# Mixing stage: w_out takes the unnormed attention outputs half by half, the token factors meet its products, and the values, tasks and places are ordered anew

## The chip, the cores and the metric

The kernel runs on one core of one Trainium2 chip. The metric is the device time of one execution in microseconds (us), as a median of several runs. PE is the matrix engine (PEld its weight loads), DVE the vector engine, ACT the activation engine, POOL the general engine, and SP issues most of the DMAs.

## What is computed

A model of five blocks, 512 tokens by 1024 features, batch 1, all in float32. The first block is the one that the change touches: a feed-forward part (ffn1), a mixing part, a second feed-forward part (ffn2), and a gated projection of a side input p (PLE). The mixing part is:

```python
u = rms_norm(h, g_mix_pre)
q_a, k_a, v_a, q_b, k_b, v_b = split(u @ w_in)          # each 512 wide, 8 heads of 64
o_a = stick_breaking_attention(q_a, k_a, v_a)
o_b = chunk_band_attention(q_b, k_b, v_b, rel_bias)
mixed = concat([rms_norm(o_a, g_out_sb), rms_norm(o_b, g_out_ch)])
h = h + rms_norm(mixed @ w_out, g_mix_post)
```

`rms_norm(o, g)` multiplies each token by one number, 1/rms over the 512 features, and each feature by its gain. Four more blocks follow (convolution, attention with forget gates, gated delta rule, sliding window); neither version differs in them.

## The kernel before

Activations lie transposed, features on the 128 partitions and 512 tokens along them, so a 1024-wide activation is eight tiles of 128x512. Every large product is made of blocks of 128x128 weights. Both sides are split into a high and a low part of the type fp32r, and a block costs three matmuls: high by high, low weights by high, high weights by low. Weights come in chunks of four blocks (256 KB) through four staging buffers `wst`; ACT makes the high part, DVE the low part. 82 places of 128x512 (`slots`) hold all other tiles, eight PSUM banks the products.

The order of all instructions is set while the program is built, by a planner in the kernel. The main line is written as plain code (`gemm`, `vproj`, `gemm_two`); the attentions are generators (`sb_pair`, `ch_pair`, each for two heads, four of each) that yield what they wait for. Between two blocks of the main line `poll` lets every generator go on that is ready by the planner's costs. `lim` says how many of them may be open at once, `room(n)` lets one start when n + 8 places are free, and a started one takes that many places for its own. ACT, DVE and POOL run the operations in the order that the planner wrote, each queue strictly in that order.

In the mixing stage the main line projects q, k and v of w_in, then w_ple_proj (which needs only p), then w_out. The names that matter:

- `project(m0, dst, half)` makes half of the values of one attention; `sb_pair` and `ch_pair` need them for their last products (`weigh`).
- `sb_pair(p)`: scores, softplus, a running sum by matmuls with a triangle (`sums`, five blocks), then `weigh`; `ch_pair(p)`: scores, softmax, transposes, `weigh`, in four steps of 128 queries.
- `mixed`: when all four pairs of an attention are done, four small matmuls (`stats`, 128x1) give the mean squares, a chain on DVE and POOL the inverse roots, four transposes (`rows`) spread them over the partitions; only then are the four tiles multiplied by gain and factor and split for w_out.
- `gemm_two("w_out", 4, 1, range(8), ...)` multiplies output tiles 0 to 4, and `need` calls `finish` on `mixed` before the first input tile is used. Tiles 5 to 7 follow in halves of 256 tokens, so that the norm behind (`post_norm`: `stats`, `rows`, then eight tiles of h and of the next input) can start on the first half.

```python
def need(k, cols):
    (t_a if k < 4 else t_b).finish()
...
gemm_two("w_out", 4, 1, range(8), Xo, evac_o, need)
```

Of the kernel before, what the change touches and what calls it, by code (L numbers as in the profile page):

```python
# [11 lines left out]
AF = mybir.ActivationFunctionType  # L12
# [5 lines left out]
P = 128  # L18
# [15 lines left out]

SWA_FIRST = (8, 9, 12, 13)
SWA_REST = (14, 15, 0, 16, 1, 17, 2, 18, 3, 19, 4, 5, 6, 7)


def _weights_plan():
# [7 lines left out]
    def mouter(items, ks):  # L47
        return [(w, k, m) for (w, m) in items for k in ks]
# [27 lines left out]
    phases.append(vproj(w, 8, 2))  # L76
    phases.append(vproj(w, 20, 2))
    phases.append(mouter([(w, m) for m in (13, 17, 2, 6)], K8))
    phases.append(vproj(w, 10, 2))
    phases.append(mouter([(w, m) for m in (3, 7, 14, 18, 15, 19)], K8))  # L80
    phases.append(vproj(w, 22, 2))
    phases.append([("w_ple_proj", k, m) for m in range(8) for k in range(2)])
    out_gemm("w_out", 1)
# [118 lines left out]
def chain_kernel(ctx, tc, xT, pT, wall, params, consts, chbias, pos, out):  # L202
# [294 lines left out]

    def quiet(t):
        return not live.get(t.name)

    def spare(n):
        return sum(map(quiet, banks.free)) >= n
# [623 lines left out]
    def soft_heads(heads, span, done, own, causal=False, ready=lambda: True):  # L1126
# [35 lines left out]
        def turn(qt, pack):  # L1162
# [7 lines left out]
            n *= len(pack)  # L1170
            A.activation(t[:, :n], pt[:, :n], AF.Copy)

        def weigh(qt):
# [11 lines left out]
        for qt in range(4):  # L1185
            if qt < 3:
                yield n
                scores(qt + 1)
            for pack in packs(qt):
                yield [pr[qt, i] for i in pack] + [1]  # L1190
                turn(qt, pack)
            if po is None:
                yield [ready, 1]
                po = PS("po")
            if qt:
                yield [ptb[qt - 1, i] for i in range(n)]
                weigh(qt - 1)
        yield [ptb[3, i] for i in range(n)]
        weigh(3)
        done(po)  # L1200

# [1 line left out]
    def mixing(S1):  # L1203
# [13 lines left out]
        va, vb = Row("va"), Row("vb")  # L1217
        v_done = set()

        def project(m0, dst, half):  # L1220


            def f(t, ps):
                A.activation(dst[t][:, 256 * half : 256 * half + 256], ps, AF.Copy, scale=S1.rc(t))

            vproj(w, m0 + 2 * half, 2, S1.X, f)
            v_done.add((m0, half))

        nones = con("nones")
        tri = T("tri", F32R)[:, : 2 * P]  # L1230
# [3 lines left out]
        ob = [None] * 4  # L1234
        na, nb = Norm(1), Norm(1)

        place = {}
        for e in range(2):
            place[0, e], place[1, e], place[3, e], place[2, e] = (3 + e, 0), (e, 0), (e, 384), (2, 256 * e)
# [9 lines left out]
        def sb_pair(p):  # L1249
# [3 lines left out]
            yield [q, k]  # L1253
            if p == 0:
                both()
            yield room(19)
            own = slots.take(19)
            sp, zc = {}, {}
            qs = [stack_q(q, e, own) for e in range(2)]
            ks = [stack_k(k, e, own) for e in range(2)]  # L1260
# [17 lines left out]
                return z  # L1278

            for b in here:  # L1280
                yield [1] + (qs + [qz] + [x for y in ks for x in y] if b == 0 else [])
# [37 lines left out]

            a = zc  # L1320
            order = (2, 3, 4, 0, 1)
            plan = sums(2)
            for b, then in zip(order, order[1:] + (None,)):
                ahead = sums(then) if then is not None else None
                yield [x for _, hl, *_ in plan for x in hl] + [1]
                z = PS("sbz")
                for i, (wt, hl, c0, o, n) in enumerate(plan):
# [10 lines left out]
                strict(a[b], b)  # L1338
            f0.clear()
            del f1, plan  # L1340
            yield [lambda: (8, p // 2) in v_done, *a.values(), 1]
            po = PS("po")
            for kt in range(4):
                for e in range(2):
# [2 lines left out]
                       tile=0.84 * (S - kt * P))  # L1347
            a.clear()
            oa[p] = T("oa", own=own)
            own.close()  # L1350
            V.tensor_copy(oa[p], po)
            del po
            na.add(oa[p], FULL)
# [1 line left out]
        def ch_pair(p):  # L1355
# [22 lines left out]
                V.tensor_copy(ob[p], po)  # L1378
                nb.add(ob[p], FULL)

            yield from soft_heads(heads, lambda qt: (0, (qt + 1) * P), done, own, ready=lambda: (20, p // 2) in v_done)

        look[0] = NEAR
        gemm(early([(w, m) for m in (0, 4, 12, 16, 1, 5)]), range(8), S1.X, evac_qk, S1.need)
        look[0] = LOOK
        lim[0] = 2
        t_s, t_c = [], []
        for p in range(4):
            t_s.append(spawn(sb_pair(p)))
            t_c.append(spawn(ch_pair(p)))  # L1390
        project(8, va, 0)
        project(20, vb, 0)
        gemm(singles(w, 13, 17, 2, 6), range(8), S1.X, evac_qk)
# [6 lines left out]
        def mixed(nrm, o, gname, k0, done, v):  # L1400
            def g():
                yield done
                v.clear()
                yield nrm.acc
                nrm.stats(FULL)
                yield nrm.rcol
# [5 lines left out]
            return spawn(g(), urgent=True)  # L1412

        t_a = mixed(na, oa, "g_out_sb", 0, t_s, va)
        t_b = mixed(nb, ob, "g_out_ch", 4, t_c, vb)

        px = [[], []]
        for k in range(2):
# [21 lines left out]

        def need(k, cols):
            (t_a if k < 4 else t_b).finish()
# [723 lines left out]
```

## Time and profile before

| | us |
|---|---|
| median of 3 runs (2142.53 to 2143.95) | 2143.01 |
| the profiled execution | 2143.3 |
| its span on the core | 2141.6 |
| PE busy in the span | 2102.8 (98%) |
| DVE, ACT, POOL busy | 1304.2, 1004.1, 291.1 |

PE is busy nearly all the time, so the time is PE's work, its idle time, and what it loses while its clock is lowered. The page's chain of what ended last is 91% PE, 4% DVE and 3% ACT. Times below, in us, count from the span's start; the mixing stage lies at about 375 to 660.

### The profile page before, as it was taken

To read this page: it belongs to the slowest core of one execution; us is meant where nothing else is said; L and a number is where in the kernel's file an instruction comes from. 1 tells how busy PE (TensorE), PEld (TensorE's weight loads), DVE (VectorE), ACT (ScalarE), POOL (GpSimd) and SP (SyncE) were. 2 spreads that over 40 slices of the span, in tenths; PEclk is the share of its full clock that TensorE was granted. 3 is DMA by queue.
4 is the path that set the end of the run, shared out by engine and by line. 5 is a ranking of instruction groups with operands and counts; after the bars stand their busy time and mean duration, and the time that the engine had idled before them with its cause. 6 is when DMAs were issued, how large, how long until landed. Compare 5 with 4: busy or idle time off the path is not lost.

```text
span 2141.6 us, 35794 instructions
## 1 busy us (share of the span) xinstructions
PE 2102.8 (98%) x13583; PEld 1771.5 (83%) x13583; DVE 1304.2 (61%) x2783; ACT 1004.1 (47%) x2189; POOL 291.1 (14%) x600
## 2 busy tenths in 40 slices
PE   8999999999989999999999999999999999999998
PEld 7888889988769888888998887888888777888776
DVE  6433455787867551444785555356567787656886
ACT  5322333687856332323652234345448546444764
POOL 0000001211113000000130001000023234222230
PEclk9999999999999999999999999999999999999999
DMA  5232332222221232323222222421222221123231
GB/s 168 98 104 94 99 118 60 85 77 72 69 94 46 95 122 73 99 99 109 95 65 95 94 98 86 153 65 60 89 62 85 66 62 55 56 89 104 75 90 55
DMA packets 105405, 186.12 MB, mean 87 GB/s; under 512 B 12392, under 2 KB 18952, under 8 KB 105232
## 3 DMA queue, kind: packets, MB, share of 16 engines
q1 hardware_dynamic: 103920, 179.62, 26.4%
q0 software_dynamic: 1312, 4.21, 0.6%
q8 instruction: 106, 1.74, 0.3%
q14 instruction: 67, 0.55, 0.1%
HBM read 179.03 MB, written 2.13 MB: 85 GB/s over the span
## 4 chain that ended last, share of the span: by engine, by line
PE 91%; DVE 4%; ACT 3%; issue 1%; DMA 1%; POOL 0%; SPq 0%; DVEq 0%; ACTq 0%; POOLq 0%
PE ps L708 89%; DVE t L404 3%; ACT t L404 3%; PE ps L713 2%; ACT L404 0%; DMA wst<-in_wall_dram 0%; POOL t L404 0%; DMA h<-in_xT_dram 0%; SPq L404 0%; DVE b L404 0%; DVE h L404 0%; POOL b L404 0%; DVE pad L404 0%; DVE a L404 0%; POOL h L404 0%
## 5 line engine op out<-in xcount | busy, mean ns | idle before, releaser
L708 PE MATMUL ps<-t,t 128*128 128x512 f32 (+4 forms) x10648 | 2026.4, 352 | 20.9 <-ACT t L404 14.7
L708 PEld LDWEIGHTS ps<-t,t 128*128 128x128 f32 (+1 forms) x10648 | 1674.8, 186 | 314.9 <-issue 22.0
L404 DVE TENSOR_TENSOR t<-wst,t 128x512 fp32r<-128x512 f32 (+1 forms) x646 | 444.3, 714 | 261.1 <-ACT t L404 259.1
L404 ACT ACTIVATE t<-t 128x512 f32<-128x512 f32 (+4 forms) x470 | 261.2, 573 | 577.2 <-DVE t L404 568.9
L404 ACT ACTIVATE t<-wst 128x512 fp32r<-128x512 f32 (+1 forms) x646 | 382.5, 622 | 116.3 <-DMA wst<-in_wall_dram 112.1
L404 DVE TENSOR_TENSOR t<-ps,t 128x512 f32<-128x512 f32 (+2 forms) x247 | 156.2, 638 | 267.2 <-PE ps L708 264.0
L404 DVE TENSOR_TENSOR t<-t,t 128x512 fp32r<-128x512 f32 (+6 forms) x387 | 236.8, 624 | 76.3 <-ACT t L404 70.7
L404 ACT ACTIVATE t<-ps 128x512 f32<-128x512 f32 (+5 forms) x357 | 140.2, 420 | 233.8 <-PE ps L708 151.5
L404 POOL TENSOR_TENSOR t<-t,t 128x512 f32<-128x512 f32 (+1 forms) x99 | 116.0, 1172 | 532.0 <-ACT t L404 462.7
L404 POOL TENSOR_TENSOR h<-h,t 128x256 f32<-128x256 f32 x40 | 32.2, 827 | 801.7 <-DVE t L404 797.3
L404 ACT ACTIVATE t<-t,a 128x257 f32<-128x257 f32 (+5 forms) x128 | 66.4, 521 | 41.9 <-DVE a L404 38.7
L404 ACT ACTIVATE t<-h,prm 128x256 fp32r<-128x256 f32 (+1 forms) x80 | 45.9, 587 | 67.2 <-DVE h L404 62.0
L404 ACT ACT_TABLE_LOAD x50 | 64.2, 1283 | 8.5 <-DVE a L404 6.4
L404 DVE SCALAR_TENSOR_TENSOR t<-pad,prm,t 128x512 f32<-128x512 f32 (+1 forms) x92 | 66.4, 731 | 1.3
L713 PE MATMUL ps<-cst,t 128*128 128x128 f32 x400 | 62.0, 275 | 2.6 <-DVE t L404 1.5
L404 DVE SCALAR_TENSOR_TENSOR t<-h,prm,t 128x256 fp32r<-128x256 f32 (+1 forms) x80 | 56.0, 725 | 8.4 <-ACT t L404 8.2
L404 ACT ACTIVATE t<-h 128x256 f32<-128x256 f32 (+2 forms) x112 | 49.6, 467 | 21.3 <-DVE h L404 19.1
L713 PEld LDWEIGHTS ps<-cst,t 128*128 128x128 f32 x400 | 47.0, 140 | 12.3 <-DVE t L404 3.9
L404 POOL TENSOR_SCALAR_AFFINE_SELECT t<-t 128x256 f32<-128x256 f32 (+2 forms) x48 | 26.6, 560 | 182.9 <-DVE t L404 103.6
L708 PEld LDWEIGHTS ps<-t 32*32 32x32 f32 (+1 forms) x2304 | 32.5, 109 | 20.3 <-DVE t L404 6.4
L404 DVE TENSOR_SCALAR t<-t,a 128x256 f32<-128x256 f32 (+3 forms) x128 | 47.1, 378 | 1.7
L404 DVE CUSTOM_DVE_ANT_0 t<-ps,t 128x128 f32<-128x128 f32 (+3 forms) x64 | 30.4, 487 | 26.2 <-PE ps L708 25.3
(93 smaller groups left out, 680.6 us busy)
## 6 DMA issues: line engine op xcount, KB each, us to landing
wst<-in_wall_dram SPq DMA_DIRECT2D x644, 256.0 KB, 2.7
t<-t SPq DMA_DIRECT2D x40, 64.0 KB, 2.0
h<-in_xT_dram SPq DMA_DIRECT2D x8, 256.0 KB, 5.3
t<-in_chbias_dram POOLq DMA_DIRECT2D x8, 256.0 KB, 3.0
t<-cdr POOLq DMA_DIRECT2D x8, 256.0 KB, 6.0
t<-gdr SPq DMA_DIRECT2D x32, 64.0 KB, 3.8
out_dram<-t SPq DMA_DIRECT2D x16, 128.0 KB, 1.8
cst<-in_consts_dram SPq DMA_DIRECT2D x1, 626.0 KB, 6.3
```

The source lines that it names most:

```text
L404: Op(self.key, lambda: f(*a, **kw), outs, ins, cost, self.prio, func, more, shared and op != "dma_start")
L708: PE.matmul(ps, lhsT, rhs, start=start, stop=stop, **kw)
L713: PE.transpose(ps, src, idn)
```

## The change

- **Places of the factors.** The generators `mixed` are gone. `apart` (one per pair) splits an attention tile as soon as its own pair is done, with the gain alone. `factors` makes the row of 1/rms for each attention and keeps it. The product of w_out with the first attention's tiles (`OUT_FIRST`) and that with the second's (`OUT_LAST`) are made apart; DVE multiplies each by its factors while it reads PSUM (`scaled`), and adds the two. Before, ACT copied the product out.
- **Order of the main line.** Values of both attentions and columns of q and k come in another order (`MIX_REST`): the second half of the first attention's values (column 10) comes last. w_ple_proj is made for six tiles ahead of w_out and for two behind it. w_out begins with input tiles 0 to 3, output tiles 0 to 4.
- **Tasks and places.** Three pairs may be open instead of two; `sb_pair` takes 18 places instead of 19 and gives back its rest before its last block of sums. A generator waits until its places are at rest (`owned`) and until the products that read an earlier tile's weights can start (`weighed`).

The weights' chunks are laid out in the new order too. Core of the diff:

```diff
+MIX_REST = (("v", 8), ("v", 20), (13, 17, 2, 6), ("v", 22), (14, 18, 3, 7, 15, 19), ("v", 10))
+PLE_FIRST, PLE_LAST = range(6), range(6, 8)
+OUT_FIRST, OUT_LAST = (0, 1, 2, 3), (4, 5, 6, 7)
...
-            yield room(19)
-            own = slots.take(19)
+            yield room(OWN)
+            own = slots.take(OWN)
...
-        lim[0] = 2
+        lim[0] = 3
...
-        project(8, va, 0)
-        project(20, vb, 0)
-        gemm(singles(w, 13, 17, 2, 6), range(8), S1.X, evac_qk)
-        project(8, va, 1)
-        gemm(singles(w, 3, 7, 14, 18, 15, 19), range(8), S1.X, evac_qk)
-        project(20, vb, 1)
+        for x in MIX_REST:
+            if x[0] == "v":
+                project(x[1], va if x[1] < 12 else vb)
+            else:
+                gemm(singles(w, *x), range(8), S1.X, evac_qk)
...
-                rb = nrm.rows(FULL)
-                for p in range(4):
-                    V.scalar_tensor_tensor(o[p], o[p], col(gname, p), rb, ALU.mult, ALU.mult)
-                    split(Xo, k0 + p, o[p], FULL)
-                    o[p] = None
+        def apart(o, gname, k0, p, t):
+            yield [t, lambda: S1.X is None]
+            split(Xo, k0 + p, o[p], FULL, col(gname, p))
+            o[p] = None
+
+        def factors(nrm, k0, ts, v):
+            yield ts
+            v.clear()
+            yield nrm.acc
+            nrm.stats(FULL)
+            yield nrm.rcol
+            nrm.rows(FULL, fac[k0][0])
...
-        gemm([([("w_ple_proj", m)], [FULL]) for m in range(8)], range(2), px, evac_p)
-        px.clear()
+        gemm(singles("w_ple_proj", *PLE_FIRST), range(2), px, evac_p)
...
+        def need(k, cols):
+            t_x[k].finish()
+
+        def scaled(dst, ps, c, k0):
+            t_f[k0].finish()
+            V0.tensor_tensor(dst[:, c], ps, fac[k0][0][:, c], ALU.mult)
+
         def put(m, ps, cols):
-            A0.activation(f[m][:, slice(*cols)], ps, AF.Copy)
+            c, t = slice(*cols), T("wo")
+            scaled(t, ps, c, OUT_LAST[0])
+            V0.tensor_tensor(f[m][:, c], f[m][:, c], t[:, c], ALU.add)
+
+        def evac_f(item, ps, cols):
+            scaled(f[item[1]], ps, slice(*cols), OUT_FIRST[0])
...
+        gemm(plain_groups("w_out")[:2], OUT_FIRST, Xo, evac_f, need)
-        gemm_two("w_out", 4, 1, range(8), Xo, evac_o, need)
-        gemm(in_halves([("w_out", m) for m in range(5, 8)]), range(8), Xo, evac_o)
+        gemm_two("w_out", 4, 1, OUT_LAST, Xo, evac_o, need)
+        for g in in_halves([("w_out", m) for m in range(5, 8)]):
+            gemm([g], OUT_FIRST, Xo, evac_f)
+            gemm([g], OUT_LAST, Xo, evac_o)
+        gemm(singles("w_ple_proj", *PLE_LAST), range(2), px, evac_p)
```

What that does to the order is shown at three places, all on PE. A row is a matmul, out<-inputs by tile (the second input is the weights), then its shape; `ps` is a PSUM bank, `t_..` a place, `cst` the constants.

**First place, the last stick-breaking pair.** Before, in order: the last three matmuls of w_ple_proj, then the sums of that pair (weights `t_2_3130`, the triangle), blocks 2 and 3, with nothing between them.

```order
L708 MATMUL ps_239<-t_8_5267,t_10_5234 128x512
L708 MATMUL ps_239<-t_8_5267,t_12_5235 128x512
L708 MATMUL ps_239<-t_12_5268,t_10_5234 128x512
L708 MATMUL ps_234<-t_13_5456,t_2_3130 128x512
L708 MATMUL ps_234<-t_15_5457,t_2_3130 128x512
L708 MATMUL ps_234<-t_7_5406,cst 128x128
L708 MATMUL ps_234<-t_9_5432,cst 128x128
L708 MATMUL ps_240<-t_13_5458,t_2_3130 128x512
L708 MATMUL ps_240<-t_14_5459,t_2_3130 128x512
L708 MATMUL ps_240<-t_14_5460,t_2_3130 128x384
L708 MATMUL ps_240<-t_10_5461,t_2_3130 128x384
```

Now the sums of a later block of the same pair stand between products of w_out (`t_9_5446` and `t_8_5447` are the high and low part of one attention tile):

```order
L721 MATMUL ps_235<-t_9_5446,t_12_5383 128x512
L721 MATMUL ps_235<-t_9_5446,t_13_5384 128x512
L721 MATMUL ps_235<-t_8_5447,t_12_5383 128x512
L721 MATMUL ps_241<-t_10_5508,t_2_3130 128x512
L721 MATMUL ps_241<-t_15_5509,t_2_3130 128x512
L721 MATMUL ps_241<-t_9_5506,t_2_3130 128x256
L721 MATMUL ps_241<-t_19_5507,t_2_3130 128x256
L721 MATMUL ps_237<-t_9_5446,t_12_5383 128x512
L721 MATMUL ps_237<-t_9_5446,t_13_5384 128x512
L721 MATMUL ps_237<-t_8_5447,t_12_5383 128x512
```

The last pairs' steps, which stood alone behind w_ple_proj, now have products of w_out between them.

**Second place, the factors of the first attention.** Before, behind the last `weigh` (64x128): the second attention's `stats` (x4), the first's `rows` (x4), and at once the first product of w_out, on a tile that the factors had to multiply first.

```order
L708 MATMUL ps_238<-t_11_5717,t_6_4042 64x128
L708 MATMUL ps_238<-t_10_5724,t_6_4042 64x128
L708 MATMUL ps_234<-cst,t_5_4208 128x1 x4
L713 MATMUL ps_239<-cst,b_170 128x128 x4
L708 MATMUL ps_237<-t_12_5776,t_9_5269 128x512
L708 MATMUL ps_237<-t_12_5776,t_11_5270 128x512
L708 MATMUL ps_237<-t_7_5777,t_9_5269 128x512
```

Now `rows` of the first attention stands between a `weigh` of the last chunk-band pair and products of w_out that do not read it:

```order
L721 MATMUL ps_241<-t_8_5734,t_8_4050 64x128 x2
L721 MATMUL ps_241<-t_8_5734,t_12_4051 64x128 x2
L726 MATMUL ps_234<-cst,b_170 128x128 x4
L721 MATMUL ps_238<-t_9_5446,t_11_5592 128x512
L721 MATMUL ps_238<-t_9_5446,t_14_5593 128x512
L721 MATMUL ps_238<-t_8_5447,t_11_5592 128x512
```

The matmuls behind the factors no longer wait for them; the evacuations of their products do.

**Third place, from w_out to ffn2.** Before, `rows` of the first half of tokens (x2) had 42 products of w_out (128x256) behind it before the first product of ffn2:

```order
L708 MATMUL ps_241<-t_9_5778,t_15_5850 128x256
L708 MATMUL ps_241<-t_10_5779,t_17_5849 128x256
L713 MATMUL ps_236<-cst,b_178 128x128 x2
L708 MATMUL ps_241<-t_14_5780,t_17_5849 128x256
L708 MATMUL ps_241<-t_14_5780,t_15_5850 128x256
```

Now three such products follow, then twelve of w_ple_proj (128x512), then ffn2:

```order
L726 MATMUL ps_240<-cst,b_178 128x128 x2
L721 MATMUL ps_239<-t_14_5910,t_8_5884 128x256
L721 MATMUL ps_239<-t_14_5910,t_14_5885 128x256
L721 MATMUL ps_239<-t_9_5911,t_8_5884 128x256
L721 MATMUL ps_235<-t_9_5427,t_12_5886 128x512
L721 MATMUL ps_235<-t_9_5427,t_13_5887 128x512
L721 MATMUL ps_235<-t_8_5428,t_12_5886 128x512
```

`rows` moved nearer to the first product of ffn2. Over the whole program PE's list is as long as before (10235 rows). On DVE the change takes out 8 multiplications of 128x512 (the norm's); it adds 22 evacuations that read PSUM and a row of factors (10 of 128x512, 12 of 128x256) and 11 additions (5 and 6). On ACT it takes out 11 copies from PSUM (5 and 6) and adds 2, of the kept factors.

## Rows read from the trace of the kernel before

**Rows 1.** The page, part 1, PE: busy us, share of the span, instructions.

```profile
PE 2102.8 (98%) x13583; PEld 1771.5 (83%) x13583; DVE 1304.2 (61%) x2783; ACT 1004.1 (47%) x2189; POOL 291.1 (14%) x600
```

**Rows 2.** What PE waited for: us in total, times, longest.

```profile
PE ps L708 <- ACT t L404: 14.7, 8, 5.4
```

**Rows 3.** Windows over the mixing stage: busy us by engine, PEclk granted clock, DMA.

```profile
430.00:562.00 132.00, 132.00 (x832) 111.48 (x831) 105.90 (x245) 97.25 (x203) 16.39 (x36) 1.00 0.26 81
562.00:676.00 114.00, 98.59 (x606) 83.09 (x605) 80.48 (x182) 75.28 (x165) 26.14 (x58) 0.93 0.19 61
```

**Rows 4.** Timeline of PE, its longest gaps: start, us, [idle before <-releaser].

```profile
580.08 0.73 PE L708 MATMUL ps<-t,t 128*128 128x512 f32 x2 [4.26 <-ACT t L404]
...
604.20 1.22 PE L708 MATMUL ps<-cst,t 128*128 128x1 f32 x8 [2.18 <-DVE t L404]
...
608.00 1.22 PE L708 MATMUL ps<-t,t 128*128 128x512 f32 x2 [1.50 <-ACT t L404]
...
625.02 0.73 PE L708 MATMUL ps<-t,t 128*128 128x512 f32 x2 [1.50 <-ACT t L404]
...
675.60 0.43 PE L713 MATMUL ps<-cst,b 128*128 128x128 f32 x2 [2.51 <-DVE b L404]
```

**Rows 5.** Windows of 10 us, the same columns.

```profile
580.00:590.00 10.00, 8.88 (x32) 7.02 (x32) 9.44 (x27) 9.41 (x23) 0.99 (x3) 0.66 0.00 0
590.00:600.00 10.00, 8.80 (x67) 5.58 (x67) 8.72 (x26) 7.90 (x20) 0.81 (x2) 1.00 0.18 54
600.00:610.00 10.00, 5.63 (x41) 4.21 (x39) 5.17 (x10) 5.23 (x9) 5.54 (x26) 0.75 0.00 1
610.00:620.00 10.00, 10.00 (x34) 8.01 (x35) 6.75 (x11) 3.15 (x5) 0.00 (x0) 0.74 0.42 137
620.00:630.00 10.00, 7.97 (x36) 6.12 (x35) 6.45 (x11) 4.20 (x7) 0.00 (x0) 1.00 0.24 77
670.00:680.00 10.00, 7.49 (x51) 7.29 (x50) 9.82 (x26) 8.11 (x19) 5.70 (x7) 0.83 0.21 75
583.30:586.60 3.30, 2.69 (x8) 2.23 (x8) 3.27 (x7) 3.27 (x7) 0.41 (x1) 0.50 0.00 0
```

**Rows 6.** Groups by form, 400 to 700 us: busy us, mean ns of one | idle before.

```profile
L404 DVE TENSOR_TENSOR t<-wst,t 128x512 fp32r<-128x512 f32 x69 | 46.6, 693 | 12.3 <-ACT t L404 11.7
L404 ACT ACTIVATE t<-wst 128x512 fp32r<-128x512 f32 x70 | 42.9, 634 | 12.6 <-DMA wst<-in_wall_dram 12.2
...
L404 DVE TENSOR_TENSOR t<-t,t 128x512 f32<-128x512 f32 x26 | 18.0, 707 | 2.8 <-ACT t L404 2.4
L404 DVE TENSOR_TENSOR t<-ps,t 128x512 f32<-128x512 f32 x25 | 16.9, 682 | 0.5 <-PE ps L708 0.4
...
L404 DVE TENSOR_TENSOR t<-t,t 128x256 f32<-128x256 f32 x27 | 11.6, 453 | 10.2 <-ACT t L404 10.2
...
L404 ACT ACTIVATE t<-ps,b 128x256 f32<-128x256 f32 x16 | 6.4, 485 | 3.5 <-PE ps L708 3.5
...
L404 DVE SCALAR_TENSOR_TENSOR t<-t,prm,ps 128x512 f32<-128x512 f32 x8 | 5.5, 742 | 4.6 <-PE ps L713 4.6
L404 DVE TENSOR_TENSOR t<-ps,t 128x256 f32<-128x256 f32 x14 | 5.4, 420 | 5.6 <-PE ps L708 5.5 <-ACT t L404 0.2
```

**Rows 7.** Timeline behind w_out, all engines: start, us, instruction.

```profile
654.96 0.38 PE L713 MATMUL ps<-cst,b 128*128 128x128 f32 x2
...
655.09 12.48 PE L708 MATMUL ps<-t,t 128*128 128x256 f32 x102
...
658.73 1.36 DVE L404 SCALAR_TENSOR_TENSOR t<-h,prm,t 128x256 fp32r<-128x256 f32 x2
...
668.93 0.50 PE L708 MATMUL ps<-cst,t 128*128 128x1 f32 x4
```

**Rows 8.** Groups by form of PE, 300 to 340 us (ffn1).

```profile
L708 PE MATMUL ps<-t,t 128*128 128x512 f32 x178 | 40.5, 389 | 0.0
```

**Rows 9.** The page, part 6, weight chunks: count, KB each, us to landing.

```profile
wst<-in_wall_dram SPq DMA_DIRECT2D x644, 256.0 KB, 2.7
```

More of the change, by code (lines that the diff above doesn't have):

```diff
@@ L75, in _weights_plan @@
     phases.append(kouter([(w, 0), (w, 4), (w, 12), (w, 16)], K8) + mouter([(w, 1), (w, 5)], K8))
[L76 to L83, printed above, removed]
+    for x in MIX_REST:
+        phases.append(vproj(w, x[1], 2) if x[0] == "v" else mouter([(w, m) for m in x], K8))
+    phases.append([("w_ple_proj", k, m) for m in PLE_FIRST for k in range(2)])
+    items = [("w_out", m) for m in range(8)]
+    phases.append(kouter(items[:4], OUT_FIRST) + mouter(items[4:5], OUT_FIRST))
+    ks = OUT_LAST
+    phases.append(kouter(items[:4], ks[:3]) + kouter(items[4:5], ks[:3]) + kouter(items[:5], ks[3:]))
+    phases.append(mouter(items[5:], OUT_FIRST + ks))
+    phases.append([("w_ple_proj", k, m) for m in PLE_LAST for k in range(2)])
     ffn("w_ffn2_gate", "w_ffn2_up", "w_ffn2_down")
@@ L499, in quiet, with owned @@
         return not live.get(t.name)
+    def owned(own, n):
+        return lambda: sum(map(quiet, own.free)) >= n
     def spare(n):
@@ L1171, in turn, with weighed @@
             A.activation(t[:, :n], pt[:, :n], AF.Copy)
+        def weighed(qt):
+            k0, n = span(qt)
+            return [ptb[qt, i] for i in range(len(heads))] + [h[3](k0 // P + j) for h in heads for j in range(n // P)]
         def weigh(qt):
@@ L1195, in soft_heads @@
             if qt:
-                yield [ptb[qt - 1, i] for i in range(n)]
+                yield weighed(qt - 1)
                 weigh(qt - 1)
-        yield [ptb[3, i] for i in range(n)]
+        yield weighed(3)
         weigh(3)
@@ L1218, in mixing, with project @@
         v_done = set()
-        def project(m0, dst, half):
+        def project(m0, dst):
+            c0 = m0 % 4 * P
             def f(t, ps):
-                A.activation(dst[t][:, 256 * half : 256 * half + 256], ps, AF.Copy, scale=S1.rc(t))
-            vproj(w, m0 + 2 * half, 2, S1.X, f)
-            v_done.add((m0, half))
+                A.activation(dst[t][:, c0 : c0 + 256], ps, AF.Copy, scale=S1.rc(t))
+            vproj(w, m0, 2, S1.X, f)
+            v_done.add(m0)
         nones = con("nones")
@@ L1235, in mixing @@
         na, nb = Norm(1), Norm(1)
+        OWN = 18
         place = {}
@@ L1280, in sb_pair @@
             for b in here:
-                yield [1] + (qs + [qz] + [x for y in ks for x in y] if b == 0 else [])
+                yield [1, owned(own, 2)] + (qs + [qz] + [x for y in ks for x in y] if b == 0 else [])
                 z = scores(b)
@@ L1321, in sb_pair @@
             order = (2, 3, 4, 0, 1)
+            yield owned(own, 2)
             plan = sums(2)
             for b, then in zip(order, order[1:] + (None,)):
+                if then is not None:
+                    yield owned(own, 4)
                 ahead = sums(then) if then is not None else None
+                if then == order[-1]:
+                    own.close()
                 yield [x for _, hl, *_ in plan for x in hl] + [1]
@@ L1340, in sb_pair @@
             del f1, plan
-            yield [lambda: (8, p // 2) in v_done, *a.values(), 1]
+            yield [lambda: 8 + p // 2 * 2 in v_done, *a.values(), 1]
             po = PS("po")
@@ L1379, in done @@
                 nb.add(ob[p], FULL)
-            yield from soft_heads(heads, lambda qt: (0, (qt + 1) * P), done, own, ready=lambda: (20, p // 2) in v_done)
+            yield from soft_heads(heads, lambda qt: (0, (qt + 1) * P), done, own, ready=lambda: 20 + p // 2 * 2 in v_done)
         look[0] = NEAR
@@ L1390, in mixing @@
             t_c.append(spawn(ch_pair(p)))
-        project(8, va, 0)
-        project(20, vb, 0)
-        gemm(singles(w, 13, 17, 2, 6), range(8), S1.X, evac_qk)
-        project(8, va, 1)
-        gemm(singles(w, 3, 7, 14, 18, 15, 19), range(8), S1.X, evac_qk)
-        project(20, vb, 1)
+        for x in MIX_REST:
+            if x[0] == "v":
+                project(x[1], va if x[1] < 12 else vb)
+            else:
+                gemm(singles(w, *x), range(8), S1.X, evac_qk)
         S1.X = None
         Xo = new_x()
[L1400 to L1406, printed above, removed]
-                rb = nrm.rows(FULL)
-                for p in range(4):
-                    V.scalar_tensor_tensor(o[p], o[p], col(gname, p), rb, ALU.mult, ALU.mult)
-                    split(Xo, k0 + p, o[p], FULL)
-                    o[p] = None
-            return spawn(g(), urgent=True)
-        t_a = mixed(na, oa, "g_out_sb", 0, t_s, va)
-        t_b = mixed(nb, ob, "g_out_ch", 4, t_c, vb)
+        fac = {k0: Row("rmix") for k0 in (0, 4)}
+        def apart(o, gname, k0, p, t):
[9 more added lines that the diff above has]
+            nrm.rows(FULL, fac[k0][0])
+        t_x, t_f = {}, {}
+        for k0, o, gname, nrm, ts, v in ((0, oa, "g_out_sb", na, t_s, va), (4, ob, "g_out_ch", nb, t_c, vb)):
+            for p in range(4):
+                t_x[k0 + p] = spawn(apart(o, gname, k0, p, ts[p]), urgent=True)
+            t_f[k0] = spawn(factors(nrm, k0, ts, v), urgent=True)
         px = [[], []]
```

4 lines of the change are left out of this document (1 added, 3 removed).

## Prediction

> **What bounds the kernel now.** I read the page first: PE is busy 98% of the span, 2102.8 of 2141.6 us [rows 1]. So the span holds 38.8 us of idle PE, and a change that leaves PE's work as it is can gain no more than the idle time and the time lost to a lowered clock, where it acts. The list of PE's waits says for whom it waits: ACT above all, 14.7 us in 8 waits, one of them 5.4 long [rows 2]. Then I cut the mixing stage in windows [rows 3]. From 430 to 562 PE is busy 132.00 of 132.00 us at full clock; there is nothing to win there, only to lose. From 562 to 676 it is busy 98.59 of 114.00, so 15.4 us of idle time lie in this stretch alone, at a mean clock of 0.93. The timeline names the places [rows 4]: 4.26 us until 580, where w_ple_proj is used up and the last stick-breaking pair's sums wait for ACT; 2.18 until 604 and 1.50 until 608, the mean squares of the second attention and the first product of w_out behind the factors; 1.50 until 625, the same for the second attention; 2.51 until 675.6, the norm behind w_out. The rest are six gaps of 0.3 to 0.7.
>
> The windows of 10 us show what follows the gaps [rows 5]: after 580, 604 and 675.6 the granted clock falls to means of 0.66, 0.75 and 0.74, and 0.83; the lower level is 0.50, that is 1.2 GHz instead of 2.4, as from 583.3 to 586.6. Busy time times what is missing to 1.00 is 8.88 x 0.34 + 5.63 x 0.25 + 10.00 x 0.26 + 7.49 x 0.17 = 3.0 + 1.4 + 2.6 + 1.3 = 8.3 us. Idle time in smaller pieces did not lower it: 1.20 us from 590 to 600 and 2.03 from 620 to 630, both at 1.00 [rows 5].
>
> **What the change can take away: 15.4 + 8.3 = 23.7 us.** Its PE list has the same matmuls in another order, so the sum is this loss less what is left of it or comes new.
>
> *The gap until 580 and the small ones until 593.* In the new order the first half of w_out (5 output tiles x 4 input tiles x 3 = 60 matmuls of 128x512) lies between the steps of the last two pairs. One takes 40.5 / 178 = 0.228 us [rows 8], so 13.7 us of work stand where 4.26 and some 2.2 us were idle. What this cover costs: two tiles of w_ple_proj (12 matmuls, 2.7 us) leave the stretch, which the 13.7 outweigh. The last stick-breaking pair also starts earlier, since a third task may be open. I take all of this gap and its 3.0 us of clock as gained.
>
> *The gaps until 604, 608 and 625.* Nothing of PE waits for factors any more but the four transposes that spread them, and these have w_out's products before and behind them. The wait moves to DVE, which multiplies while it reads PSUM. If the factors are late, four or five of the eight banks stay full until they come, and the heads have the rest; the products behind them bridge that. I take these 5.2 us and their 4.0 us of clock as gained, with up to 2 us (the 2.18 of one such chain [rows 4]) as the upper bound of what returns.
>
> *What comes new.* (a) The last values come late now, and the products of the third stick-breaking pair stand right behind them, with no other work between. ACT must first copy the values out, four times 0.485 us [rows 6]; one is enough for the first product. I take 0.6, between 0.5 and 1.9 (all four). (b) Behind `rows` of the first half of tokens stood 42 products, now 3 of 128x256 and 12 of 128x512. The first tile of ffn2's input was done about 659.4, half of 1.36 behind 658.73, so 4.4 us behind `rows` at 654.96 [rows 7]. The cover is now 0.38 + 3 x 0.122 + 12 x 0.228 = 3.5 us (0.122 is 12.48 / 102 [rows 7]). Left: 0.9, between 0 (if the chain is done early) and 2.7 (if two more pairs of evacuation and addition, 0.420 + 0.453 each [rows 6], stand ahead of it on DVE). (c) The next norm's mean squares came 14.0 us behind `rows` (668.93 less 654.96 [rows 7]); ahead of them PE now has 75 x 0.122 + 12 x 0.228 = 11.9 us of work and the 0.9 of (b). Left: 1.2, between 0 and the 2.51 that the norm costs now. (d) The second half's tiles and the weights that queue on DVE behind this norm: DVE is busy 9.82 of 10 us there [rows 5]. No row prices it; between 0 and 2.5, I take 0.8, nearer to nothing, since today's order shows no wait there beside that of 2.51. These pieces are all shorter than the gaps behind which the clock fell, so I charge no clock for them.
>
> *DVE and ACT.* DVE gets 10 x 0.682 + 12 x 0.420 + 5 x 0.707 + 6 x 0.453 less 8 x 0.742 = 12.2 us more [rows 6]; ACT gets less. At cost nothing, as long as PE covers it: from 430 to 676 DVE is busy 105.9 + 80.5 = 186.4 of 246 us [rows 3]; with the change it is 198.6 in some 226, or 88%. If that cover fails, see the second rival. The other edits (places, waits of tasks, order of columns) move work inside 430 to 562, where PE is never idle; they cost nothing while it has other products ready, which the order shows.
>
> *Sum.* Against the profiled execution: 2143.3 - 23.7 + 0.6 + 0.9 + 1.2 + 0.8 = 2123.1. That execution lies 0.3 above the median of 2143.0, so I say **2123.0**. The forecast's own range: with none of (a) to (d) 2119.3; with half again of each and a returned gap 2126.
>
> **The rivals.**
>
> *The clock still falls.* (a) to (d) lie in two groups, three of them within some 20 us. Idle pieces of 2.18 and 2.51 us were enough for a fall, at a price of 1.3 (the last) to 4.0 us (the one at 604). If the pieces behind w_out add up to such a one, the time is 2124 to 2127. Against it: the stretches 590 to 600 and 620 to 630 [rows 5]. The Trainium skill (TensorE: Matmul & The Clock Gate, "A second HAM failure mode: psum-queue depth-cycling") says that frequent short idles between groups of matmuls can also make the clock swing; by that rule the sum would be some 2126, and the two stretches at 1.00 do not show it.
>
> *DVE becomes the bound.* It works its queue in order, and 88% over 226 us leaves little for waits. It reaches 18.2 of 20 us from 580 to 600 [rows 5], which speaks against; but there it has a whole pair's work at hand. It decides from the point where DVE cannot be kept at 88%: at 85% the stretch takes 198.6 / 0.85 = 234 us instead of 226, and the time is 2131. Waits of PE for PSUM banks that DVE has not read would show it.
>
> *Slower: the places run short.* A third open pair may hold 18 + 14 + 18 = 50 of the 82 places where two held 33, beside values and outputs. Weights get the rest: each chunk needs two places, and one that is fetched late shows its whole way, 2.7 us to land [rows 9], 0.634 on ACT and 0.693 on DVE [rows 6], 4.0 us. Some 69 chunks pass between 400 and 700 us [rows 6]. Five late ones eat the gain; from seven the kernel is slower, and with eight it takes 2155. Against it: a pair starts only when 8 places more than it needs are free, four chunks' worth, and now gives back what it can earlier.
>
> *It does not do what it says.* The last pair's chain (scores, softmax, transposes, products) may be as long as before and merely have its gaps behind w_out's first half: if the second half of w_out waits for it as the first half did, the time stays near 2143. Against it: it starts earlier, and only the last 8 products and w_out's other half need it.
>
> **How the numbers follow.** About 0.2%, 4.3 us, can be told from no change. Forecast 0.62 (2119 to 2126); clock 0.10 (2124 to 2127); DVE 0.20 (2127 to 2134); no effect 0.04; slower 0.04. The first three are faster: 0.92; same 0.04; slower 0.04. The range 2119 to 2131 takes in the forecast, the clock and about half of the DVE case, a little over 0.8.
>
> **What would show it.** Right: PE idle under 5 us from 430 to the start of ffn2, clock 1.00 there, and no wait of several us on ACT; DVE near 88%. Step by step: idle of about 0.6 us before the third pair's products, about 0.9 before ffn2's first and about 1.2 before its mean squares. Wrong: gaps over 2 us between the heads of the last pairs (the order does not cover the chain), a clock under 1.00 in several windows, waits for PSUM readers on DVE, weight loads that end PE's gaps, or any idle time between 430 and 540.

## The result, and the profile after

The changed kernel takes 2122.34 us (median of 4 runs, 2121.26 to 2122.96); the kernel before took 2142.77 on the same chip. The ratio is 0.9903, with a 95% interval of 0.9886 to 0.992. The prediction was 2123.0, with a range of 2119 to 2131. The profiled execution took 2122.96.

The page's first line, to be held against [rows 1], and the span:

```profile
span 2121.3 us, 35806 instructions
PE 2095.4 (99%) x13583; PEld 1767.1 (83%) x13583; DVE 1313.3 (62%) x2808; ACT 1000.5 (47%) x2180; POOL 293.1 (14%) x600
```

The span is 20.3 us shorter. PE's busy time fell by 7.4 (2102.8 to 2095.4) with as many matmuls; that is the clock, which falls nowhere in the stage any more. The rest, 12.9, is idle time: 38.8 became 2121.3 - 2095.4 = 25.9. The list of waits says the same; ACT's 14.7 us [rows 2] are halved, and the 5.4 that stays is a wait at the program's start, until 5.44:

```profile
PE ps L721 <- ACT t L413: 7.4, 7, 5.4
PE ps L721 <- DVE t L413: 6.6, 10, 1.4
```

Windows over the mixing stage, columns as in [rows 3]:

```profile
430.00:562.00 132.00, 132.00 (x850) 112.25 (x848) 111.67 (x259) 104.78 (x218) 18.55 (x42) 1.00 0.24 73
562.00:676.00 114.00, 111.42 (x758) 98.16 (x757) 98.46 (x228) 75.93 (x166) 31.59 (x59) 1.00 0.26 81
430.00:656.00 226.00, 224.26 (x1449) 191.65 (x1448) 193.43 (x446) 167.61 (x354) 42.81 (x91) 1.00 0.26 80
620.00:630.00 10.00, 10.00 (x86) 10.00 (x85) 9.99 (x25) 6.83 (x17) 0.00 (x0) 1.00 0.06 22
630.00:640.00 10.00, 10.00 (x75) 9.52 (x74) 10.00 (x30) 4.75 (x11) 1.44 (x2) 1.00 0.45 131
```

From 562 to 676 PE was busy 98.59 us at a mean clock of 0.93; now it is 111.42 at 1.00. The last two rows matter later: from 620 to 640 DVE is busy 19.99 of 20 us. PE's timeline from 540 to 680 holds five gaps in all, 0.60 + 0.21 + 0.83 + 0.43 + 0.41 = 2.5 us; the rows without a bracket are steps that wait for nothing:

```profile
562.83 3.04 PE L721 MATMUL ps<-t,t 128*64 128x512 f32 x18 [0.60 <-ACT t L413]
...
598.19 1.66 PE L721 MATMUL ps<-t,t 128*128 128x512 f32 x6 [0.21 <-ACT t L413]
...
636.60 0.38 PE L726 MATMUL ps<-cst,b 128*128 128x128 f32 x2
...
641.13 8.66 PE L721 MATMUL ps<-t,t 128*128 128x256 f32 x70 [0.83 <-DVE t L413]
649.63 0.95 PE L721 MATMUL ps<-cst,t 128*128 128x1 f32 x8
...
658.85 1.82 PE L721 MATMUL ps<-t,t 128*128 128x256 f32 x13 [0.43 <-DVE t L413]
661.08 7.22 PE L721 MATMUL ps<-t,t 128*128 128x256 f32 x58 [0.41 <-DVE t L413]
```

### The profile page after: what moved, and what is told of

The parts are those of the page before. It is cut to its first block, busy times and chain, and to the rows that moved or that the text cites. A ratio compares the mean times of both kernels' runs of the same rounds, so it can differ in the third digit from the quotient of the medians.

```text
span 2121.3 us, 35806 instructions
## 1 busy us (share of the span) xinstructions
PE 2095.4 (99%) x13583; PEld 1767.1 (83%) x13583; DVE 1313.3 (62%) x2808; ACT 1000.5 (47%) x2180; POOL 293.1 (14%) x600
## 4 chain that ended last, share of the span: by engine, by line
PE 90%; DVE 4%; ACT 3%; issue 1%; DMA 1%; POOL 0%; SPq 0%; DVEq 0%; ACTq 0%; POOLq 0%
PE ps L721 88%; DVE t L413 4%; ACT t L413 3%; PE ps L726 2%; POOL t L413 0%; ACT L413 0%; DMA wst<-in_wall_dram 0%; DMA h<-in_xT_dram 0%; SPq L413 0%; DVE h L413 0%; POOL b L413 0%; DVE b L413 0%; DVE pad L413 0%; DVE a L413 0%; POOL h L413 0%
## 5 line engine op out<-in xcount | busy, mean ns | idle before, releaser
L413 ACT ACTIVATE t<-t 128x512 f32<-128x512 f32 (+5 forms) x462 | 256.2, 573 | 571.2 <-DVE t L413 563.5
L413 DVE TENSOR_TENSOR t<-ps,t 128x512 f32<-128x512 f32 (+1 forms) x269 | 167.3, 630 | 264.0 <-PE ps L721 258.4
L413 ACT ACTIVATE t<-ps 128x128 f32<-128x128 f32 (+5 forms) x348 | 137.1, 419 | 234.4 <-PE ps L721 145.6
L413 POOL TENSOR_SCALAR b<-b 128x4 f32<-128x4 f32 (+3 forms) x84 | 22.7, 270 | 172.1 <-DVE b L413 167.3
```

What stands on the lines that cost most here:

```text
L413: Op(self.key, lambda: f(*a, **kw), outs, ins, cost, self.prio, func, more, shared and op != "dma_start")
```

## The experiments

Times are medians, and "before" is the kernel before on the same chip (2142.8 to 2143.7 in all runs). The first question was which part of the change brings the 20.4 us: the products of w_out that lie between the last pairs' steps, or the order and tasks that make those pairs early.

### The parts apart

**The old number of tasks.** `lim[0] = 2` instead of 3.

> The changed kernel with two attention pairs open at once instead of three; all else stays. Theory A (w_out's first half is the cover: its 60 matmuls, 13.7 us, fill the gaps of the last pairs): 2122 to 2126, some idle time at most where the last stick-breaking pair starts later. Theory B (the last pairs' earlier start is what gains): the wait of about 4 us on ACT behind w_ple_proj comes back with its lowered clock, 2128 to 2132.

Measured: 2127.4 (2126.19 to 2130.1), ratio 0.9929 (0.9914 to 0.9944), 5.1 more than the changed kernel. The gap ahead of the third pair's products is 0.97, six more of up to 0.97 lie between 566 and 594, and three of 0.74, 1.33 and 1.28 at the start of ffn2. The clock stays 1.00. The time lies between the ranges of the two theories.

**The old order of values and columns.**

```diff
-MIX_REST = (("v", 8), ("v", 20), (13, 17, 2, 6), ("v", 22), (14, 18, 3, 7, 15, 19), ("v", 10))
+MIX_REST = (("v", 8), ("v", 20), (13, 17, 2, 6), ("v", 10), (3, 7, 14, 18, 15, 19), ("v", 22))
```

> The changed kernel with values and columns of q and k in the order of before (column 10 of the values ahead of the columns 3 to 19, column 22 last), three tasks open. Theory A: 2122 to 2126; the last chunk-band pairs wait for their values, w_out's first half covers it. Theory B: the last stick-breaking pair starts later, 2128 to 2132.

Measured: 2126.32 (2125.54 to 2126.81), ratio 0.9921 (0.9905 to 0.9938), 4.0 more. This too lies between the two ranges. PE's timeline has a gap of 2.18 at 567.28, ahead of a chunk-band pair's transposes, and the window behind it is at the lower level:

```profile
570.00:575.00 5.00, 5.00 (x14) 4.03 (x14) 5.00 (x16) 5.00 (x12) 2.61 (x7) 0.50 0.00 0
```

**Old w_out in the new order.** The factors, `need` and the products of w_out as before, w_ple_proj's eight tiles ahead of it; the new order, three tasks and places stay.

```diff
-        gemm(plain_groups("w_out")[:2], OUT_FIRST, Xo, evac_f, need)
...
-        gemm_two("w_out", 4, 1, OUT_LAST, Xo, evac_o, need)
...
+        gemm_two("w_out", 4, 1, range(8), Xo, evac_o, need)
```

> The kernel of before in w_out (factors ahead of the products, one sum over eight input tiles, w_ple_proj whole ahead of it), with the change's order of values, three tasks and its places. Theory A: the last pairs start earlier, but the factor chains still stop PE; the gap until 580 (4.26 us) and its clock (3.0) shrink, the 5.2 us of the factors with their 4.0 of clock and the 2.5 of the norm stay: 2131 to 2136. Theory B: most of the gain is here, 2123 to 2127.

Measured: 2135.32 (2133.92 to 2135.69), ratio 0.9963 (0.995 to 0.9976). The order, the third task and the places together, without the new w_out, bring 7.6 us, as A said. What is left are the waits for the factors and the norm, with the clock at 0.50 from 615 to 620:

```profile
612.80 0.65 PE L721 MATMUL ps<-cst,b 128*128 128x128 f32 x4 [3.56 <-POOL b L408]
614.95 29.71 PE L716 MATMUL ps<-t,t 128*128 128x512 f32 x159 [1.50 <-ACT t L408]
667.37 0.43 PE L721 MATMUL ps<-cst,b 128*128 128x128 f32 x2 [2.51 <-DVE b L408]
```

**New w_out in the old order.** The old `MIX_REST` and `lim[0] = 2` together; the products of w_out and the factors as in the change.

> The change in w_out alone (attention tiles split as their pair ends, factors at the products, halves, two tiles of w_ple_proj behind), with the order of values of before and two tasks. Theory A: 2123 to 2128, nearly the whole gain. Theory B: the last pairs still come too late, the gap until 580 stays, 2132 to 2138.

Measured: 2133.94 (2132.74 to 2135.56), ratio 0.9959 (0.9944 to 0.9973). The new w_out, with the changed places but neither the order nor the third task, brings 9.0 us. The theory that its first half covers the chain whenever the pair starts (A) asked for at most 2128, and falls; the time is in B's range, but instead of one gap of 4.26 there are seven of up to 1.55. PE's timeline from 582 to 599, and the stretch as one window:

```profile
584.03 0.50 PE L721 MATMUL ps<-t,t 128*128 128x512 f32 x1 [1.55 <-DVE t L413]
...
586.90 1.13 PE L721 MATMUL ps<-t,t 128*128 128x512 f32 x4 [0.90 <-DVE t L413]
589.17 0.97 PE L721 MATMUL ps<-t,t 128*128 128x512 f32 x4 [1.14 <-DVE t L413]
590.37 1.77 PE L721 MATMUL ps<-t,t 128*128 128x512 f32 x7 [0.23 <-DVE t L413]
593.27 2.96 PE L721 MATMUL ps<-t,t 128*64 128x384 f32 x18 [1.12 <-POOL t L413]
```

```profile
582.00:599.00 17.00, 10.31 (x53) 6.18 (x51) 16.77 (x32) 13.49 (x27) 4.28 (x10) 1.00 0.27 79
```

With two more, the last ahead of 598.48, 6.7 us of PE's time are idle in this stretch, and DVE is busy 16.77 of 17. In PE's list the 18 matmuls of the last pair's sums stand within 20 rows; in the changed kernel they are spread over 84 rows, with products of w_out between them. Here 36 products of w_out, all that its first four output tiles have with the three attention tiles that were ready, stand ahead of the sums, so the cover was used up before the chain needed it.

So 9.0 + 7.6 = 16.6 of the 20.4 us come from either part alone, and some 3.8 only from both. Both runs keep the changes to the places (18 instead of 19, `owned`, `weighed`), so what these bring or cost is counted in both.

### Throughput of DVE, or the length of the chain

In that window DVE is nearly full, so the gaps could be DVE's throughput (C1), or the length of the last pair's chain (C2), in which each step waits for the one before.

**DVE relieved, chain lengthened.** The new w_out in the old order, with the low parts of the last pair's sums made on POOL.

```diff
-                V.tensor_tensor(lo[:, :n], t[:, :n], hi[:, :n].bitcast(F32), ALU.subtract)
+                (G if p == 3 else V).tensor_tensor(lo[:, :n], t[:, :n], hi[:, :n].bitcast(F32), ALU.subtract)
```

> e4 (w_out's part of the change alone) with the low parts of the last stick-breaking pair's sums made on POOL instead of DVE: 7 subtractions, some 4.8 us less for DVE, each about 0.5 us longer on POOL (1.17 against 0.69). e4 has 6.7 us of idle PE between 584 and 599, waiting for DVE, which is busy 9.88 and 9.78 of 10 us there. Theory C1 (DVE's throughput is the bound there): idle time falls by 2 to 4 us, 2130 to 2132. Theory C2 (the latency of the last pair's chain is the bound, so that only an earlier start helps): seven longer steps cost up to 3.5 us, 2134 to 2138.

Measured: 2138.55 (2136.3 to 2139.64, 10 runs), ratio 0.9977 (0.9967 to 0.9986): 4.6 slower than the same kernel with these on DVE, and above both ranges. One such step takes 1420 ns on POOL, where DVE takes 681 for the same shape (groups by form of the two kernels, 575 to 605 us):

```profile
L413 POOL TENSOR_TENSOR t<-t,t 128x512 fp32r<-128x512 f32 x6 | 8.5, 1420 | 0.8 <-ACT t L413 0.7
```

```profile
L413 DVE TENSOR_TENSOR t<-t,t 128x512 fp32r<-128x512 f32 x6 | 3.9, 681 | 0.0
```

DVE falls from 16.77 of 17 us (99%) to 17.80 of 20 (89%, from 582 to 602), and PE now waits for POOL, up to 2.57 us. But the run lengthened more than the steps that it moved. With the subtractions on POOL, several of DVE's other operations take longer there, among those that read no PSUM: from 575 to 605 us the low part of a weight chunk takes 964 ns instead of 705, while an evacuation of 128x512 takes 686, where it took 684. The row with the old place of the subtractions, then this run's:

```profile
L413 DVE TENSOR_TENSOR t<-wst,t 128x512 fp32r<-128x512 f32 x5 | 3.5, 705 | 0.1
```

```profile
L413 DVE TENSOR_TENSOR t<-wst,t 128x512 fp32r<-128x512 f32 x5 | 4.7, 964 | 0.1
```

And the loss is not idle time: over the whole span PE is idle for 33.2 us (2135.0 less 2101.8) against 33.0 (2131.0 less 2098.0), while its busy time is 3.8 longer, at a granted clock of 0.50 from 586 to 602. So less load on DVE did not help, but the run does not tell DVE's throughput from the chain by itself.

**The last pair late, all else as changed.**

```diff
+            if p == 3:
+                yield lambda: S1.X is None
             yield room(OWN)
```

> The changed kernel, but the last stick-breaking pair may take its places only when the last values have been projected (about 562 us); order of the main line, w_out in halves and three tasks stay. Theory C2 (the last pairs' chain is long, and only its early start lets w_out's first half cover it): PE runs out of products again, idle pieces on ACT and DVE between 570 and 605 of 8 to 15 us with a lowered clock behind the longest, 2133 to 2142. Rival (the cover of 60 matmuls is enough by itself): 2122 to 2125.

Measured: 2137.41 (2136.46 to 2139.89, 10 runs), ratio 0.9974 (0.9964 to 0.9983), 15.1 us more than the changed kernel. The large gaps of before come back in nearly their size, 3.62 and 2.17 where there were 4.26 and 2.18. Over 30 us DVE has time (18.16), but in these two gaps, the second and third window, it is busy 3.22 of 3.60 and 2.07 of 2.20:

```profile
595.01 0.79 PE L721 MATMUL ps<-t,t 128*128 128x512 f32 x1 [3.62 <-ACT t L413]
...
610.17 1.60 PE L721 MATMUL ps<-cst,t 128*128 128x1 f32 x8 [2.17 <-DVE t L413]
```

```profile
590.00:620.00 30.00, 21.53 (x80) 15.01 (x79) 18.16 (x37) 16.29 (x31) 6.98 (x23) 0.77 0.04 11
591.40:595.00 3.60, 0.00 (x0) 0.00 (x0) 3.22 (x10) 3.60 (x9) 1.29 (x3) 0.78 0.00 0
608.00:610.20 2.20, 0.03 (x1) 0.04 (x1) 2.07 (x4) 1.24 (x2) 0.00 (x0) 1.00 0.00 0
```

So whether the length of the chain or the throughput of DVE and ACT, which work on it, bounds such a stretch is not shown; that it comes from a late pair is. How late the pair is can be read in two places. Its first operation on POOL (`qz`, 128x256), in the kernel before, the changed one, the new w_out in the old order, and this run:

```profile
543.79 0.32 POOL L404 MEMSET t<- 128x256 f32 x1 [5.92 <-PE ps L708]
535.71 0.31 POOL L413 MEMSET t<- 128x256 f32 x1
548.70 0.32 POOL L413 MEMSET t<- 128x256 f32 x1 [14.06 <-DVE t L413]
579.80 0.32 POOL L413 MEMSET t<- 128x256 f32 x1
```

And four matmuls of its first block of sums, in the same order:

```profile
580.65 0.68 PE L708 MATMUL ps<-t,cst 128*128 128x128 f32 x4
565.71 0.61 PE L721 MATMUL ps<-t,cst 128*128 128x128 f32 x4
584.36 0.61 PE L721 MATMUL ps<-t,cst 128*128 128x128 f32 x4
597.92 1.05 PE L721 MATMUL ps<-t,cst 128*128 128x128 f32 x4
```

So this run starts the pair 44 us later than the changed kernel and 36 later than the kernel before, and while it waits it counts as one of the three open pairs; the 15.1 us are not the price of the 8.1 us by which the change starts the pair earlier. What the three with the new w_out show together is that its first half covers the chain only if the chain comes to its sums while products are left. In the old order the pair had begun, at 548.70, and still came to its sums only at 584, behind the 36 products. An early start is not all that the order gives, either: in the old order with three tasks the pair starts at 521.95 and sums at 543.39, earlier than in the changed kernel, and the time is 4.0 more.

### DVE's margin

**Every scaled evacuation twice.** In `scaled`, the multiplication is issued twice; the result is the same.

> The changed kernel with every evacuation of w_out made twice on DVE (22 more operations, 10 x 0.68 + 12 x 0.42 = 11.9 us of DVE). Theory A (PE covers DVE in the mixing stage except between w_out and ffn2, where DVE is busy 9.99 of 10 us): the second copies of the six halves behind output tile 4 (12 x 0.42 = 5 us) show there in part, +3 to +6 us and perhaps a lowered clock; the others are free: 2125 to 2130. Rival (DVE is the bound of the whole stage): all 12 us show, 2134.

Measured: 2134.75 (2133.36 to 2135.19), ratio 0.9957 (0.9942 to 0.9972), 12.4 more, for 9.4 us of work on DVE (1322.7 less 1313.3 busy). The number is that of the rival, 2134, and above theory A's range. But the place is not the whole stage: up to 630 PE's gaps are as without it. Then:

```profile
644.52 1.01 PE L721 MATMUL ps<-cst,t 128*128 128x1 f32 x4 [3.65 <-DVE t L413]
...
654.20 9.65 PE L721 MATMUL ps<-t,t 128*128 128x256 f32 x58 [4.54 <-DVE t L413]
```

```profile
562.00:630.00 68.00, 67.10 (x403) 54.95 (x402) 58.71 (x121) 46.41 (x97) 11.84 (x36) 1.00 0.30 90
640.00:660.00 20.00, 9.70 (x42) 8.11 (x42) 19.67 (x52) 13.66 (x36) 11.29 (x15) 0.57 0.19 54
```

DVE has room ahead of the norm and none from 620 on. Up to 620 it is busy 2.2 us more than in the changed kernel (48.75 against 46.59 from 562), and PE has lost nothing; some 7.2 of the 9.4 us fall behind 620. There the added time shows as gaps, 10.7 us from 630 on where the changed kernel has 1.7, and as clock: PE's busy time is 2.9 longer.

**DVE relieved.** Three ways: the additions of `put` on POOL, but for the last tile; the first products copied out by ACT (this leaves the first attention's factors out of the computation); the additions into h, four tiles on POOL instead of five.

```diff
-            V0.tensor_tensor(f[m][:, c], f[m][:, c], t[:, c], ALU.add)
+            (V0 if m == 7 else Eng(nc.gpsimd, "POOL", -1)).tensor_tensor(f[m][:, c], f[m][:, c], t[:, c], ALU.add)
```

> The changed kernel with 9 of the 11 additions of the two halves of w_out on POOL (all but the last output tile's two): 5 x 0.71 + 4 x 0.45 = 5.3 us less for DVE just ahead of ffn2. Theory C1 (DVE's throughput is what is left between w_out and ffn2: 1.67 us of idle PE): some of it goes, 2121 to 2122.5. Theory C2 (the norm's chain): no change or up to 1 us more, 2122 to 2123.5.

```diff
-            scaled(f[item[1]], ps, slice(*cols), OUT_FIRST[0])
+            t_f[OUT_FIRST[0]].finish()
+            A0.activation(f[item[1]][:, slice(*cols)], ps, AF.Copy)
```

> The changed kernel with the products of w_out's first half copied by ACT instead of multiplied by the first attention's factors on DVE: those factors are left out of the result. 11 operations, 5 x 0.68 + 6 x 0.42 = 5.9 us less for DVE, as much more for ACT. Theory C1: the 1.67 us between w_out and ffn2 shrink, 2120.5 to 2122. Theory C2: they stay, 2122 to 2123.

```diff
-ON_POOL = (1, 2, 4, 6, 7)
+ON_POOL = (1, 3, 5, 7)
```

> The changed kernel with four instead of five of the eight additions to h of each norm behind a product on POOL (tiles 1, 3, 5, 7 instead of 1, 2, 4, 6, 7), everywhere in the program: POOL takes 0.83 us for one, DVE 0.60. Theory C2 (the norm's chain is the bound behind w_out, and POOL's additions are its slowest step): 0.5 to 1 us less idle time there, and as much behind the four other such norms, 2119 to 2122. Theory C1 (DVE's throughput): more idle time, 2122.5 to 2124.

Measured: 2122.15 (2121.65 to 2122.53), 2125.24 (2124.18 to 2126.23) and 2123.65 (2121.48 to 2124.34); ratios 0.9901 (0.9886 to 0.9915), 0.9915 (0.99 to 0.993) and 0.9906 (0.9891 to 0.9921). None is told apart from the changed kernel as faster; the second is 2.9 us slower, above both of its ranges. The first lies in both of its ranges. The third lies in that of DVE's throughput (C1), but is only 1.3 us from the changed kernel, less than its own runs are apart. With the additions on POOL, which take 4.7 us from DVE (1308.6 busy), the gaps ahead of ffn2 and in it are 0.65, 0.27 and 1.46, 2.4 in all instead of 1.67. With ACT's copies the planner orders the rest anew, and two larger ones stand there:

```profile
643.75 6.07 PE L721 MATMUL ps<-t,t 128*128 128x256 f32 x36 [1.91 <-DVE t L413]
659.79 0.40 PE L726 MATMUL ps<-cst,b 128*128 128x128 f32 x2 [2.82 <-DVE b L413]
```

So more work on DVE costs at once, and less brings nothing that can be measured. What ends the last 1.67 us, the length of the norm's chain or the order in DVE's queue, stays open.

**More of w_ple_proj behind w_out.** `PLE_FIRST, PLE_LAST = range(4), range(4, 8)`.

> The changed kernel with four tiles of w_ple_proj behind w_out instead of two (and four ahead). Theory A (the piece left between w_out and ffn2 is the norm's chain less its cover): the 0.83 us before ffn2's first product go, since 12 more matmuls, 2.7 us, stand there; what is taken ahead of w_out comes back as up to 2 us of idle time among the last pairs: 2121 to 2124. Rival (the piece is DVE's queue, not the chain): the 0.83 us stay or move to the products behind it: 2122 to 2125.

Measured: 2128.99 (2128.33 to 2129.55), ratio 0.9932 (0.9915 to 0.9948), 6.7 more. It misses what was expected: a longer cover behind w_out did not shorten the waits there. Gaps of 0.97, 0.53 and 0.21 come back at the last pairs, and at the start of ffn2 stand 0.80, 1.32 and

```profile
660.35 0.40 PE L726 MATMUL ps<-cst,b 128*128 128x128 f32 x2 [3.06 <-DVE b L413]
```

Why the norm's chain came later was not tried further.

### What a gap costs in clock

**Probes.** In ffn1 and ffn2, seven times each, a chain of copies on DVE and a 128x1 matmul behind it that PE must wait for, from one copy to fifteen.

```diff
+PROBE = {4: 0, 6: 2, 8: 4, 10: 6, 12: 8, 14: 10, 16: 14}
...
+                if j in PROBE:
+                    y = T("probe")
+                    V0.tensor_copy(y, ps)
+                    for _ in range(PROBE[j]):
+                        V0.tensor_copy(y, y)
+                    poll([y])
+                    pr = PS("probe")
+                    mm(pr[:, :1], y[:, :P], meanc[:, 0:1], tile=220)
```

> The changed kernel with small matmuls in ffn1 and ffn2 that wait for a chain of DVE copies, at output tiles 4, 6, 8, 10, 12, 14 and 16 of the gate, with 1, 3, 5, 7, 9, 11 and 15 copies: idle pieces of PE of about 1, 2, 2.5, 3, 4, 4.5 and 6 us, far apart from each other. Nothing else is added. Theory (single pieces as short as those that the change leaves cost only themselves, longer ones lower the clock behind them): the granted clock stays at 1.00 behind the pieces up to 1.5 us and falls to 0.50 behind all over 3.5 us, for some 3 us of lost time each. Rival (short pieces lower it too): a fall behind the piece of 1 us as well. Some 45 us slower in all.

Measured: 2209.84 in one run, 87.5 more than the changed kernel where 45 were expected; the gaps came out longer than meant, up to 7.71 us and 57 in all. Two gaps of one size, and the 10 us that begin at each probe's matmul, in ffn1 and ffn2 in turn (the third window is behind 3.10 us, the fourth behind 7.71):

```profile
85.77 0.38 PE L722 MATMUL ps<-cst,t 128*128 128x1 f32 x2 [2.18 <-DVE t L414]
763.34 0.38 PE L722 MATMUL ps<-cst,t 128*128 128x1 f32 x2 [2.18 <-DVE t L414]
```

```profile
85.70:95.70 10.00, 9.93 (x45) 8.23 (x46) 5.08 (x9) 3.19 (x6) 0.00 (x0) 1.00 0.27 81
...
763.30:773.30 10.00, 9.96 (x38) 8.08 (x39) 3.50 (x6) 2.36 (x5) 0.00 (x0) 0.83 0.27 80
790.30:800.30 10.00, 9.96 (x38) 8.12 (x39) 3.43 (x6) 1.47 (x4) 0.00 (x0) 0.83 0.23 79
```

```profile
289.50:299.50 10.00, 9.93 (x31) 8.02 (x32) 2.66 (x6) 0.00 (x0) 0.00 (x0) 0.67 0.26 81
```

Behind a gap of 0.79 us the clock stayed at 1.00 both times; behind 2.18 it stayed once and fell once; behind 3.10, 4.02 and 4.95 the mean was 0.83 each time, 10 x 0.17 = 1.7 us; behind 5.87 it was 0.77 and behind 7.71 it was 0.67, 3.3 us. So neither the theory's 3 us behind every longer gap nor the rival's fall behind 1 us came out.

## Why the prediction was right, point by point

**What can be taken away.** Right, and for a reason that was half told. None of the gaps of [rows 4] is left, so the 15.4 us of idle time went as forecast. The text took the 13.7 us of products as enough, and put the third task beside it as one more reason; of the other edits (places, waits, order of columns) it said that they cost nothing, since PE is never idle from 430 to 562. That stretch is indeed still full, 132.00 of 132.00. But the order and the tasks decide how far the last pair has come when the cover runs: without them the gain is 9.0, and with that pair held back by 44 us it is 5.8 (2143.16 on that chip less 2137.41). The number came out right because the whole change was costed at once. Which of `OWN`, `owned` and `weighed` is needed was not tried.

**The clock.** The text summed 8.3 us; 7.4 came back by PE's busy time. This term was 0.9 too large, and why stays open: the mean clock over windows of 10 us is not the reason, since the same sum over windows of 1 us gives 8.7 (2.9 behind 580, 4.0 behind 604, 1.7 behind 675.6). The granted clock is 1.00 in every window of the stage.

**(a) Values copied out:** 0.6 forecast, 0.60 measured, at 562.83. **(b) First product of ffn2:** 0.9 forecast, 0.83 measured. It starts 4.5 us behind `rows` (641.13 less 636.60), where the text took 4.4 from [rows 7]. **(c) Mean squares of the next norm:** 1.2 forecast, nothing measured. This is the term that was mis-sized: the text asked for 14.0 us from `rows`, as before, and they now come 13.0 behind it (649.63 less 636.60) with no wait, eight at once instead of four, since those of w_out's second half stand with them. **(d) Second half and weights:** 0.8 forecast, 0.43 + 0.41 = 0.84 measured. That a row of before gave no price for it makes the agreement partly luck. The gap of 0.21 at 598.19 was not forecast.

**The sum.** By the measured terms: 2143.3 - 15.4 - 7.4 + 2.5 = 2123.0, against 2122.96. The clock was 0.9 too high and the residue 1.0 too high; that the two misses cancel is luck.

**DVE and ACT.** The text took 198.6 of 226 us, 88%; measured are 193.43, 86%. There is no gap between 430 and 562, and none for the factors: the 0.21 ends with ACT, and the product behind it writes the bank (`ps_238`) that the last transposes stood in, out of which ACT copies just before.

**The rivals.** *DVE becomes the bound* did not happen, but the kernel stands at its edge: a mean of 86% hides 20 us at 100%, and the doubled evacuations cost 12.4 us from that place on. The text's measure of it, the mean over 226 us, was the wrong one to watch. *The clock still falls* did not happen here: the pieces are at most 0.83 us, and the granted clock is 1.00 behind all of them. As a mechanism it is real, with no sharp price. The new w_out in the old order has pieces of up to 1.55 us, 6.7 in 17, at a clock of 1.00. With the low parts on POOL the pieces ahead of the fall and at it were 0.30, 1.26 and 0.58 us, and from 586 to 602 the clock was at its lower level:

```profile
582.00:585.50 3.50, 1.88 (x8) 1.15 (x8) 3.47 (x7) 1.54 (x4) 2.62 (x4) 1.00 0.21 66
586.00:602.00 16.00, 10.67 (x27) 6.00 (x29) 13.83 (x29) 11.08 (x25) 10.38 (x14) 0.50 0.21 67
```

The rule of the Trainium skill that the text weighed (TensorE: Matmul & The Clock Gate, "A second HAM failure mode: psum-queue depth-cycling"), that frequent short idles can make the clock swing, agrees with the second of these and not with the first. *The places run short* did not happen: no gap of PE from 430 to 680 was ended by a DMA, and none is over 0.83. *It does not do what it says* is, in part, what the kernel with the late last pair looks like, 2137.41; this kernel does what it says.

## What to carry to other kernels

Independent work placed behind a chain covers it only if the chain comes to its waits while that work lasts; that it has begun is not enough. Move the last serial task forward together with the cover, look at both in the order, and count the two as one edit. Where a wait is moved from PE to another engine's queue, look at that engine's fullest 10 or 20 us, not at its mean over the stage; in the stretch at 100% here, added work was paid in full and with clock on top, while freeing it brought nothing that could be measured. Price a gap on PE with its clock: the probes' gaps from 3.10 us on each cost 1.7 us or more besides themselves. When work moves to POOL, look at what DVE's own operations take beside it.

## What was not expected

- The same gap of 2.18 us lowered the clock once and left it once, in ffn1 and in ffn2 of one execution.
- Idle pieces of 0.30 to 1.26 us, close together, were followed by a fall, while 6.7 us of pieces of up to 1.55 in another order of the same work were not.
- 9.4 us of added DVE work cost 12.4 us of time: some 7.2 of it fell on the one place without slack, and a lowered clock came on top; 4.7 us less on DVE brought 0.2, which is within the scatter.
- With eight subtractions moved from DVE to POOL, some of DVE's other operations took longer: 964 ns instead of 705 for the low part of a weight chunk.
